# Inputs of the down projection in other buffers, forms and norm products of the feed-forward stage at other places in the order

## The chip, the core and the metric

The kernel runs on one core of one Trainium2 chip. Its engines are TensorE (PE in the profile; its weight loads are listed apart as PEld), VectorE (DVE), ScalarE (ACT) and GpSimd (POOL); SyncE (SP) only issues DMAs, as ScalarE and GpSimd also can. Each engine works through its own list of instructions in order, and waits where an instruction needs what another engine has not finished. The time is the device time of one execution in microseconds, the median of several runs.

## The reference

Two layers of a bidirectional encoder trunk in float32, on 512 tokens of width 1024:

```python
for l in range(DEPTH):                                   # DEPTH = 2
    h = rms_norm(x, attn_norm_g[l])
    proj = h @ w_in[l]
    c_q, c_kv, k_rope, gq, gk, gv, pool_in, gate_logits = split_columns(proj, IN_SIZES)
    o_mla = mla_branch(...)                              # latent attention, 8 heads
    o_gqa = gqa_branch(...)                              # grouped-query attention, 8 heads on 2
    o_pool = pool_branch(...)                            # centred means over 2/4/8/16 tokens
    merged = gates[0] * (o_mla @ w_branch_mla[l]) + gates[1] * (o_gqa @ w_branch_gqa[l]) \
             + gates[2] * (o_pool @ w_branch_pool[l])
    x = x + merged @ w_out[l]
    hf = rms_norm(x, ffn_norm_g[l])
    u = depthwise_conv(hf @ ffn_w_up[l], ffn_conv_w[l], ffn_conv_b[l])   # 1024 -> 2 x 2816, width 3
    u_gate, u_val = u[..., :D_FF], u[..., D_FF:]
    x = x + (silu(u_gate) * u_val) @ ffn_w_down[l]       # 2816 -> 1024
```

`rms_norm(x, g)` is `x * rsqrt(mean(x*x) + 1e-6) * g` over the width.

## The kernel before

**Numbers.** A float32 product is made of three matmuls of a faster format: each operand is split into a high part and the remainder, and `mm3` (L529) multiplies high by high, high by low and low by high into one accumulation in PSUM. So every operand has two tiles: `HH` and `HL` for the normed input, `wh` and `wl` for weights, `act` twice (or `ah` and `al`) for the input of the down projection.

**Order.** Nothing is scheduled by the compiler: the Python code writes every engine's list itself, and the order in which it writes is the order in which each engine works. To choose it, the code keeps a clock (`Clock`): it estimates when each instruction would end, and a chain of steps (`chain(..., after=t)`) is written when the estimated time reaches its place. Whatever has the earlier estimated time stands earlier in an engine's list. The real waits are semaphores.

**Memory.** Tiles lie in pools that are opened one after the other and get their byte offsets in that order. Pool `sp` has 47 plain slots of 2048 bytes per partition for nearly everything; `wp` has 5 wide ones of 2112 bytes (for the means); `sm` has the small ones; `mp` has 4 buffers of 6144 bytes, used in attention and, in the feed-forward stage, as 12 places of 2048 bytes for inputs of the down projection. A slot that is taken again makes its first writer wait for its last reader. In the built program `mp` is last and its places begin at 204640, 206688 and so on, that is at 32 past a multiple of 64 bytes; the plain slots begin at 93824 and lie, like `HH` and `HL`, at multiples of 128; the wide buffers begin at 190080, 192192, 194304, 196416 and 198528, of which the second and the fourth lie 64 past a multiple of 128.

**From the output projection to the feed-forward stage.** The output projection gives 8 columns of 128 features, each an accumulation of 24 matmuls 512 tokens wide (operands `mgh`, `mgl`). Behind each column m a chain stands: VectorE adds it to the residual (`XM`), ScalarE makes `HH` and the squares, VectorE makes `HL`, GpSimd adds the squares. Then the feed-forward stage needs two things of it.

- The norm: `norm_begin` transposes the sum of squares (`sqT`) and reduces it on VectorE (`prt`). `norm_finish` puts one small product of `prt` on TensorE (into `ps_S`), and from it come the factors `fac`, `rt` and the row `rbc` by which results are multiplied later. It is called at every step of the first accumulations, and writes the product at the first call where the estimate says that `prt` has been ready for `D_SUM` (2.0 us; `D_FIRST`, 2.4, for the very first norm, generation 0). Generations 1 and 3 are the two feed-forward norms, 2 is the norm ahead of the second layer.
- The forms: the up projection is made in two ways. The first 5 of 22 chunks are plain (10 accumulations of 24 matmuls 512 wide, 8 row blocks of three). The other 17 use a scheme with seven products in place of eight for each two by two blocks (forms 11, 12, 1, 22, 2, 4, 3), 256 tokens wide. It needs sums and differences of row blocks: `build_forms(q)` for the quad q of row blocks 2q and 2q + 1 scales the two (`hn`), makes four half-wide sums (`tt`) on VectorE, and splits them into `tf`. It is called behind each odd column, and its chain starts 2.0 us of estimated time later.

**Down projection.** The 22 chunks are in five groups of 5, 5, 5, 4 and 3. While one group's forms are multiplied, the products of the group before with the down weights (`act` or `ah`/`al`, 512 wide) are dealt out between them in bursts of some 6 to 9 matmuls. The last group's stand alone at the end of the layer. Of each group, chunks go to the 12 places of `mp` as far as they reach (groups of 5, 1, 5, 1 and 3 chunks, two places each); the other 4 and 3, called the spare ones here, have their high part in a wide buffer (`ah`) and their low part in a plain slot (`al`). 8 columns by 22 chunks make 176 down products of three matmuls in a layer.

Of the kernel before, what the change touches and what calls it, by code (L numbers as in the profile page):

```python
# [11 lines left out]
F32R = mybir.dt.float32r  # L12
# [6 lines left out]
P = 128  # L19
T = 512  # L20
# [10 lines left out]
WIDE = 528  # L31
# [26 lines left out]
D_SUM, D_FIRST = 2.0, 2.4  # L58
# [150 lines left out]
class Clock:  # L209
# [37 lines left out]
    def done(self, *key):  # L247
        self.ready[key] = self.fin + self.SEM

    def need(self, *keys):  # L250
        for k in keys:
            while k not in self.ready:
                self.pop()
            self.to(self.ready[k])
# [4 lines left out]
    def chain(self, *steps, after=0.2):  # L259

        def go(n, source=None):
            if n == len(steps):
                return
            keys, fn = steps[n] if isinstance(steps[n], tuple) else ((), steps[n])
            late = [self.ready.get(k, self.now + 0.5) for k in keys]
            if late and max(late) > self.now:
                self.at(max(late) - self.now, lambda: go(n))
                return
            self.fin, self.source, self.last = self.now, source, None
            fn()  # L270
            source, self.source = self.last, None
            self.at(max(0.0, self.fin - self.now), lambda: go(n + 1, source))
        self.at(after, lambda: go(0))
# [65 lines left out]
def trunk(ctx: ExitStack, tc: tile.TileContext, x, w, prm, gb, cst, out):  # L339
    nc = tc.nc  # L340
    ctx.enter_context(tc.manual_schedule())
    ck = Clock()
    at, need, done, chain = ck.at, ck.need, ck.done, ck.chain
# [3 lines left out]
    cp = ctx.enter_context(tc.tile_pool(name="cp", bufs=1))  # L347
    rawp = ctx.enter_context(tc.tile_pool(name="rawp", bufs=RAW))
    hlp = ctx.enter_context(tc.tile_pool(name="hlp", bufs=LA + 3))
    sp = ctx.enter_context(tc.tile_pool(name="sp", bufs=NSLOT))  # L350
    wp = ctx.enter_context(tc.tile_pool(name="wp", bufs=NWIDE))
    sm = ctx.enter_context(tc.tile_pool(name="sm", bufs=2))
# [3 lines left out]
    uid = [0]  # L356

    def slot(name, dt=F32):
        uid[0] += 1
        t = sp.tile([P, SLOT], dt, tag="s", name=f"{name}_{uid[0]}")  # L360
        return t
# [5 lines left out]
    def small(name, shape, dt=F32, bufs=2):  # L367
        uid[0] += 1
        t = sm.tile(shape, dt, tag=name, name=f"{name}_{uid[0]}", bufs=bufs)
        return t  # L370
# [4 lines left out]
    def ps(tag):  # L375
        while not banks[tag]:
            ck.pop()
        ck.to(heapq.heappop(banks[tag]))
        uid[0] += 1
        t = pp.tile([P, T], F32, tag=tag, name=f"ps_{tag}_{uid[0]}", bufs=nbank[tag])  # L380
        return t
# [8 lines left out]
    def free(tag):  # L390
        heapq.heappush(banks[tag], ck.fin + ck.SEM)

    def f(ap):
        return ap.bitcast(F32)
# [130 lines left out]
    def mm(o, lhsT, rhs, start, stop, again=False):  # L525
        PE.matmul(o, lhsT=lhsT, rhs=rhs, start=start, stop=stop, skip_group_check=again)  # L526
        n = rhs.shape[-1]
        ck.to(ck.now + (n / 2400.0 + 0.0133 if st["ffn"] else max(0.107, n / 2370.0)))
# [20 lines left out]
    keep = cp.tile([P, 1], F32, tag="keep", name="keep")  # L549


    mp = ctx.enter_context(tc.tile_pool(name="mp", bufs=4))

    prms = []
    for l in range(L):
        t = cp.tile([P, NPRM], F32, tag=f"prm{l}", name=f"prm{l}")
# [60 lines left out]

    def norm_finish(gen, out, force=False):

        if gen not in parts or not (force or ck.ready.get(("prt", gen), 1e9) + (D_SUM if gen else D_FIRST) <= ck.now):  # L620
            return
        need(("prt", gen))
        s2 = ps("S")
        mm(s2[:, :16], C[:, C_GRP:C_GRP + P], parts.pop(gen), True, True)
        a, a4 = small("fac", [P, 16]), small("fac4", [P, 16])
        rt, rbc = out["rt"], out["rbc"] = small("rt", [P, 4]), slot("rbc")

        def mean():
            V.tensor_scalar(a, s2[:, :16], 1.0 / D, EPS, ALU.mult, ALU.add)
            free("S")  # L630

        def tokens():
            V.tensor_tensor(a4, a, C[:, C_SEL:C_SEL + 16], ALU.mult)
            V.tensor_reduce(rt, a4.rearrange("p (b g) -> p b g", g=4), AX.X, ALU.add)
            done("rt", gen)

        def rows():
            V.transpose(rbc[:, :T].rearrange("p (j r) -> p j r", r=32), bc(a.unsqueeze(2), [P, 16, 32]))
            done("rbc", gen)

        chain(mean, lambda: G.tensor_tensor(a, a, bc(mhalf, [P, 16]), ALU.pow), tokens, rows, after=0.3)
# [13 lines left out]
    parts = {}  # L655

    def bc(ap, shape):
        return ap.to_broadcast(shape)
# [26 lines left out]
    def layer(l, sq, xsrc):  # L685
# [3 lines left out]
        def col(i):  # L689
            return pr[:, i:i + 1]  # L690
# [899 lines left out]
        def build_forms(q):  # L1590
            a, b = slot("hn")[:, :T], slot("hn")[:, :T]
            lo, hi = slice(0, 256), slice(256, 512)
            t = (slot("tt")[:, :T], slot("tt")[:, :T])

            def whole():
                for k, z in ((2 * q, a), (2 * q + 1, b)):
                    V.tensor_scalar(z, XM[:, k, :], col(PRM_FG + k), None, ALU.mult)

            def sums():
                V.tensor_tensor(t[0][:, lo], a[:, hi], a[:, lo], ALU.subtract)  # L1600
                V.tensor_tensor(t[1][:, lo], b[:, hi], a[:, hi], ALU.subtract)
                V.tensor_tensor(t[0][:, hi], b[:, hi], t[0][:, lo], ALU.subtract)
                V.tensor_tensor(t[1][:, hi], b[:, lo], t[0][:, hi], ALU.subtract)

            def halves_of(name):
                i, h = {"1": (0, lo), "2": (0, hi), "3": (1, lo), "22": (1, hi)}[name]
                d = slot("tf", F32R)[:, :T]
                forms[name, q] = d[:, lo], d[:, hi]

                def low():  # L1610
                    V.tensor_tensor(d[:, hi], t[i][:, h], f(d[:, lo]), ALU.subtract)
                    done("tf", l, name, q)
                return [lambda: A.activation(d[:, lo], t[i][:, h], AF.Copy), low]

            for name, k, h in (("11", 2 * q, lo), ("12", 2 * q + 1, lo), ("4", 2 * q + 1, hi)):
                forms[name, q] = HH[:, k, h], HL[:, k, h]
                done("tf", l, name, q)
            chain(whole, sums, *[z for name in ("1", "2", "22", "3") for z in halves_of(name)], after=2.0)

        for m in range(KC):  # L1620
            tag = tags[m % 3]
# [28 lines left out]
        def keep_act(c):  # L1650
            g = next(i for i, (c0, c1) in enumerate(groups) if c0 <= c < c1)
            i = c - groups[g][0]
            n = 2 * (PLACE[g] + i)
            if n < 2 * ROOM:
                return places[n], places[n + 1]
            uid[0] += 1
            return wp.tile([P, WIDE], F32R, tag="w", name=f"ah_{uid[0]}")[:, :T], slot("al", F32R)[:, :T]

        def convolve(c, part, u):
            ci = c + part * FC  # L1660
# [353 lines left out]
```

## Time and profile before

| | us |
|---|---|
| median of 3 runs (lowest, highest) | 1552.65 (1552.56, 1552.98) |
| the profiled execution, device time | 1550.6 |
| its span, first to last instruction | 1548.8 |
| TensorE busy | 1542.1 |
| VectorE, ScalarE, GpSimd busy | 1156.3, 1066.5, 775.3 |
| granted TensorE clock, mean | 1.000 |

In a row of a timeline the first number is the start in us from the span's start, the second the duration of the row's instructions, then engine, line, operation, and output tile <- input tiles with their shapes; in brackets stands the idle time just before and what ended it. Matmuls overlap in the pipeline: a 512-wide one lasts 0.39 us, but the next starts some 0.23 us after it. So the distance from start to start is what counts. In a view of groups the two numbers behind the bar are the busy time in us and the mean duration of one in ns; in a view of waits they are the total, the number of times and the longest.

### The profile page before, as it was taken

To read this page: it belongs to the slowest core of one execution; us is meant where nothing else is said; L and a number is where in the kernel's file an instruction comes from. 1 tells how busy PE (TensorE), PEld (TensorE's weight loads), DVE (VectorE), ACT (ScalarE), POOL (GpSimd) and SP (SyncE) were. 2 spreads that over 40 slices of the span, in tenths; PEclk is the share of its full clock that TensorE was granted. 3 is DMA by queue.
4 is the path that set the end of the run, shared out by engine and by line. 5 is a ranking of instruction groups with operands and counts; after the bars stand their busy time and mean duration, and the time that the engine had idled before them with its cause. 6 is when DMAs were issued, how large, how long until landed. Compare 5 with 4: busy or idle time off the path is not lost.

```text
span 1548.8 us, 24353 instructions
## 1 busy us (share of the span) xinstructions
PE 1542.1 (100%) x8265; PEld 1341.3 (87%) x8265; DVE 1156.3 (75%) x1936; ACT 1066.5 (69%) x1994; POOL 775.3 (50%) x828
## 2 busy tenths in 40 slices
PE   9999999999999999999999999999999999999999
PEld 8888888888878999999898888888888899999997
DVE  6877886776687887877756678868667778888785
ACT  5557875877657877777644577758776677777772
POOL 3984886753453323222488648776535432222223
PEclk9999999999999999999999999999999999999999
DMA  5432344658968878886434323447598688787853
GB/s 203 123 120 82 88 123 141 162 128 207 225 164 195 197 169 181 197 192 143 128 128 131 111 75 92 125 144 175 117 216 213 169 205 186 180 187 177 212 116 102
DMA packets 138509, 241.26 MB, mean 156 GB/s; under 512 B 30864, under 2 KB 53392, under 8 KB 138384
## 3 DMA queue, kind: packets, MB, share of 16 engines
q1 hardware_dynamic: 91152, 162.93, 34.0%
q0 software_dynamic: 42336, 76.56, 28.8%
q8 instruction: 65, 1.06, 0.3%
q10 hardware_dynamic: 4896, 0.21, 0.2%
q14 instruction: 60, 0.49, 0.1%
HBM read 149.41 MB, written 13.63 MB: 105 GB/s over the span
## 4 chain that ended last, share of the span: by engine, by line
PE 92%; DVE 3%; DMA 2%; ACT 1%; issue 1%; POOL 1%; SPq 0%; ACTq 0%; POOLq 0%; DVEq 0%
PE ps_acc L526 40%; PE ps_AV L526 17%; PE ps_ST L526 15%; PE ps_S L526 10%; PE ps_mi L526 9%; DMA raw<-w 1%; DVE tf L307 1%; ACT wh L300 0%; SPq L862 0%; POOL wl L307 0%; DVE ctl L311 0%; DVE win L307 0%; ACT mx L300 0%; DVE wl L307 0%; POOL fac L307 0%
## 5 line engine op out<-in xcount | busy, mean ns | idle before, releaser
L438 POOL DMA_DIRECT2D wl<-raw x192 | 172.4, 903 | 383.1 <-ACT sx L300 163.7
L307 POOL TENSOR_TENSOR wl<-raw,wh 128x512 fp32r<-128x512 f32 (+2 forms) x171 | 219.9, 1294 | 179.4 <-ACT wh L300 171.7
L300 ACT ACTIVATE wh<-raw 128x512 fp32r<-128x512 f32 (+2 forms) x453 | 266.3, 605 | 55.6 <-DMA raw<-w 13.2
L438 POOL DMA_DIRECT2D fl<-raw x102 | 89.0, 873 | 155.2 <-ACT fl L300 62.6
L526 PE MATMUL ps_acc<-HH,wh 128*128 128x512 f32 x416 | 163.2, 392 | 0.5 <-DVE XM L311 0.4
L526 PE MATMUL ps_acc<-HL,wh 128*128 128x512 f32 x416 | 162.8, 391 | 0.3 <-DVE HL L311 0.3
L526 PE MATMUL ps_acc<-HH,wl 128*128 128x512 f32 x416 | 162.7, 391 | 0.0
L311 DVE SCALAR_TENSOR_TENSOR a<-u,prm,a 128x511 f32<-128x511 f32 x176 | 133.5, 761 | 33.5 <-ACT a L300 32.5
L300 ACT ACTIVATE wl<-wh 128x512 fp32r<-128x512 f32 x192 | 120.6, 628 | 6.1
L315 DVE TENSOR_REDUCE nm<-ps_S 128x1 fp32r<-128x512 f32 x128 | 87.8, 686 | 44.6 <-PE ps_S L526 43.7
L300 ACT ACTIVATE a<-u,prm 128x512 f32<-128x512 f32 x88 | 71.2, 811 | 57.2 <-DVE u L307 57.1
L526 PE MATMUL ps_acc<-tf,wh 128*128 128x256 f32 x544 | 100.1, 282 | 0.0
L526 PEld LDWEIGHTS ps_acc<-tf,wh 128*128 128x128 f32 x544 | 88.5, 189 | 6.2
L526 PEld LDWEIGHTS ps_acc<-HH,wh 128*128 128x128 f32 x416 | 78.4, 188 | 16.6 <-issue 0.7
L526 PEld LDWEIGHTS ps_acc<-HH,wl 128*128 128x128 f32 x416 | 78.2, 188 | 16.8
L526 PEld LDWEIGHTS ps_acc<-HL,wh 128*128 128x128 f32 x416 | 78.3, 188 | 16.6 <-DVE HL L311 0.6
L307 DVE TENSOR_TENSOR wl<-raw,wh 128x512 fp32r<-128x512 f32 (+2 forms) x91 | 66.2, 729 | 22.9 <-ACT wh L300 22.7
L526 PE MATMUL ps_AV<-HH,wh 128*128 128x256 f32 (+1 forms) x248 | 82.2, 331 | 0.0
L526 PE MATMUL ps_AV<-HH,wl 128*128 128x256 f32 (+1 forms) x248 | 82.1, 331 | 0.0
L526 PE MATMUL ps_AV<-HL,wh 128*128 128x256 f32 (+1 forms) x248 | 82.1, 331 | 0.0
L526 PE MATMUL ps_acc<-tf,wl 128*128 128x256 f32 x272 | 76.7, 282 | 0.0
L307 DVE TENSOR_TENSOR pl<-ps_ST,ph 128x512 fp32r<-128x512 f32 x86 | 58.3, 682 | 15.6 <-ACT ph L300 11.4
(426 smaller groups left out, 4975.3 us busy)
## 6 DMA issues: line engine op xcount, KB each, us to landing
raw<-w SPq DMA_DIRECT2D x160, 512.0 KB, 3.9
wl<-raw POOLq DMA_DIRECT2D x188, 256.0 KB, 4.4
raw<-w SPq DMA_DIRECT2D x140, 256.0 KB, 4.4
fl<-raw POOLq DMA_DIRECT2D x102, 256.0 KB, 5.6
raw<-w SPq DMA_DIRECT2D x14, 384.0 KB, 3.0
XM<-x SPq DMA_DIRECT2D x16, 256.0 KB, 4.5
dtq<-tr SPq DMA_DIRECT2D x16, 192.0 KB, 2.0
dtk<-tr SPq DMA_DIRECT2D x16, 192.0 KB, 3.3
```

Source lines behind the costliest of these rows:

```text
L300: return self.eng.activation(out, in_, func, **k)
L307: return self.eng.tensor_tensor(out, *a)
L311: return self.eng.scalar_tensor_tensor(out, *a)
L315: return self.eng.tensor_reduce(out, in_, *a, **k)
L438: nc.gpsimd.dma_start(f(lo), r, accum_op=ALU.add)
L526: PE.matmul(o, lhsT=lhsT, rhs=rhs, start=start, stop=stop, skip_group_check=again)
```

## The change

It has four edits in three parts. `mp` is opened ahead of the plain slots; in the built program its places then begin at 93824, 95872 and so on, all at multiples of 128, and the plain slots behind it at 118400, also at multiples of 128. The spare chunks' high parts (`ah`) go to plain slots too. The product of a feed-forward norm (generations 1 and 3) is written once `prt` has been ready for 2.4 us of estimated time, not 2.0. And the chain of `build_forms` starts 8.0 us after the norm step for quads 2 and 3, not 2.0.

```diff
     hlp = ctx.enter_context(tc.tile_pool(name="hlp", bufs=LA + 3))
+    mp = ctx.enter_context(tc.tile_pool(name="mp", bufs=4))
     sp = ctx.enter_context(tc.tile_pool(name="sp", bufs=NSLOT))
...
-    mp = ctx.enter_context(tc.tile_pool(name="mp", bufs=4))
-
...
     def norm_finish(gen, out, force=False):
 
-        if gen not in parts or not (force or ck.ready.get(("prt", gen), 1e9) + (D_SUM if gen else D_FIRST) <= ck.now):
+        if gen not in parts or not (force or ck.ready.get(("prt", gen), 1e9) + (D_FIRST if gen in (0, 1, 3) else D_SUM) <= ck.now):
             return
...
-            chain(whole, sums, *[z for name in ("1", "2", "22", "3") for z in halves_of(name)], after=2.0)
+            chain(whole, sums, *[z for name in ("1", "2", "22", "3") for z in halves_of(name)], after=2.0 if q < 2 else 8.0)
...
             if n < 2 * ROOM:
                 return places[n], places[n + 1]
-            uid[0] += 1
-            return wp.tile([P, WIDE], F32R, tag="w", name=f"ah_{uid[0]}")[:, :T], slot("al", F32R)[:, :T]
+            return slot("ah", F32R)[:, :T], slot("al", F32R)[:, :T]
```

What moves, first on VectorE, at the end of the first layer's output projection. `XM<-ps_ST` is the residual of the last column, `HL` the low part of a normed row block, `hn`, `tt` and `tf` belong to the third quad's forms, `sqT` and `prt` to the norm. Before:

```order
L311 SCALAR_TENSOR_TENSOR XM<-ps_acc_4604,XM 128x512
L311 SCALAR_TENSOR_TENSOR HL<-XM,prm_91,HH 128x512
L319 TENSOR_SCALAR hn_4671<-XM,prm_91 128x512
L319 TENSOR_SCALAR hn_4672<-XM,prm_91 128x512
L307 TENSOR_TENSOR tt_4673<-hn_4671 128x256
L307 TENSOR_TENSOR tt_4674<-hn_4672,hn_4671 128x256
L307 TENSOR_TENSOR tt_4673<-hn_4672,tt_4673 128x256
L307 TENSOR_TENSOR tt_4674<-hn_4672,tt_4673 128x256
L311 SCALAR_TENSOR_TENSOR XM<-ps_ST_4660,XM 128x512
L307 TENSOR_TENSOR tf_4675<-tt_4673,tf_4675 128x256
L311 SCALAR_TENSOR_TENSOR HL<-XM,prm_91,HH 128x512
```

And now:

```order
L311 SCALAR_TENSOR_TENSOR XM<-ps_acc_4604,XM 128x512
L311 SCALAR_TENSOR_TENSOR HL<-XM,prm_91,HH 128x512
L311 SCALAR_TENSOR_TENSOR XM<-ps_ST_4660,XM 128x512
L311 SCALAR_TENSOR_TENSOR HL<-XM,prm_91,HH 128x512
L319 TENSOR_SCALAR hn_4671<-XM,prm_91 128x512
L319 TENSOR_SCALAR hn_4672<-XM,prm_91 128x512
L307 TENSOR_TENSOR tt_4673<-hn_4671 128x256
L307 TENSOR_TENSOR tt_4674<-hn_4672,hn_4671 128x256
L307 TENSOR_TENSOR tt_4673<-hn_4672,tt_4673 128x256
L307 TENSOR_TENSOR tt_4674<-hn_4672,tt_4673 128x256
L331 STREAM_TRANSPOSE sqT_4712<-sq_4307 128x512
L315 TENSOR_REDUCE prt_4713<-sqT_4712 128x16
```

The residual and the low part of the last row block now stand ahead of the third quad's scalings and sums, and the norm's transpose and reduction ahead of that quad's four `tf`. The second layer shows the same.

On TensorE, in the second accumulation of the feed-forward stage, `ps_S<-prt` is the norm's product. Before:

```order
L526 MATMUL ps_ST_4778<-HH,wl_4691 128x512
L526 MATMUL ps_S_4814<-prt_4719,C 128x16
L526 MATMUL ps_ST_4778<-HH,wh_4690 128x512
L526 MATMUL ps_ST_4778<-HL,wh_4690 128x512
L526 MATMUL ps_ST_4778<-HH,wl_4691 128x512
```

And now:

```order
L527 MATMUL ps_ST_4770<-HL,wh_4690 128x512
L527 MATMUL ps_ST_4770<-HH,wl_4691 128x512
L527 MATMUL ps_S_4813<-prt_4713,C 128x16
L527 MATMUL ps_ST_4770<-HH,wh_4690 128x512
L527 MATMUL ps_ST_4770<-HL,wh_4690 128x512
L527 MATMUL ps_ST_4770<-HH,wl_4691 128x512
```

Two more row blocks, six matmuls, now stand ahead of the product, with one row block behind it in the accumulation where there were three. Apart from the product, TensorE's list is the same throughout; GpSimd's and SyncE's lists are the same; ScalarE's changes only at the same two places, where the next weight splits now come ahead of the forms' copies.

## The prediction

> **What bounds the kernel now.** I read the page first (engines, granted clock, chain), then the view of waits for TensorE, then the timelines of TensorE, VectorE and ScalarE around the two places where a feed-forward stage begins, then TensorE's groups by shape in the down projections, and last the load queue.
>
> ```profile
> span 1548.8 us, 24353 instructions
> PE 1542.1 (100%) x8265; PEld 1341.3 (87%) x8265; DVE 1156.3 (75%) x1936; ACT 1066.5 (69%) x1994; POOL 775.3 (50%) x828
> PE 92%; DVE 3%; DMA 2%; ACT 1%; issue 1%; POOL 1%; SPq 0%; ACTq 0%; POOLq 0%; DVEq 0%
> ```
>
> The reader is to see that TensorE is the bound: it is busy over the whole span and makes up 92% of the chain that ended last. A change moves the time only where it closes a gap between two matmuls, or shortens the distance from one matmul's start to the next. The view of waits (total, times, longest) names the gaps near this change:
>
> ```profile
> PE ps_S L526 <- DVE prt L315: 0.6, 2, 0.4
> PE ps_acc L526 <- DVE HL L311: 0.3, 1, 0.3
> ```
>
> The one wait for `HL` is in the first layer: the last row block (7) of the normed input comes late to the first feed-forward accumulation. TensorE there, start of each matmul in the first column:
>
> ```profile
> 425.67 0.39 PE L526 MATMUL ps_ST<-mgh,wh 128*128 128x512 f32 x1
> ...
> 426.12 0.39 PE L526 MATMUL ps_ST<-mgh,wl 128*128 128x512 f32 x1
> ...
> 430.43 0.39 PE L526 MATMUL ps_acc<-HH,wh 128*128 128x512 f32 x1
> ...
> 432.19 0.50 PE L526 MATMUL ps_acc<-HL,wh 128*128 128x512 f32 x1 [0.28 <-DVE HL L311]
> ...
> 432.77 0.39 PE L526 MATMUL ps_ST<-HH,wh 128*128 128x512 f32 x1
> ```
>
> From 425.67 to 430.43 lie 21 matmuls: 4.76 / 21 = 0.2267 us from start to start, the undisturbed distance of a 512-wide matmul here. From 430.43 to 432.77 lie six, which should take 1.36 us and take 2.34: 0.98 us are lost.
>
> **Part 1, forms of the later quads scaled 8.0 after the norm step, not 2.0.** Nothing is added; VectorE's order changes. Why `HL` was late:
>
> ```profile
> 425.46 0.88 DVE L319 TENSOR_SCALAR hn<-XM,prm 128x512 f32<-128x512 f32 x2
> 426.26 1.52 DVE L307 TENSOR_TENSOR tt<-hn 128x256 f32<-128x256 f32 x1
> 427.70 1.51 DVE L307 TENSOR_TENSOR tt<-hn,hn 128x256 f32<-128x256 f32 x1
> 429.13 0.87 DVE L307 TENSOR_TENSOR tt<-hn,tt 128x256 f32<-128x256 f32 x2
> 429.92 0.68 DVE L311 SCALAR_TENSOR_TENSOR XM<-ps_ST,XM 128x512 f32<-128x512 f32 x1
> ...
> 431.39 0.75 DVE L311 SCALAR_TENSOR_TENSOR HL<-XM,prm,HH 128x512 fp32r<-128x512 f32 x1 [0.46 <-ACT HH L300]
> ...
> 434.95 0.70 DVE L331 STREAM_TRANSPOSE sqT<-sq 128x512 f32<-128x512 f32 x1
> ...
> 435.89 0.67 DVE L315 TENSOR_REDUCE prt<-sqT 128x16 f32<-128x512 f32 x1
> ...
> 437.27 0.41 DVE L307 TENSOR_TENSOR tt<-hn 128x256 f32<-128x256 f32 x1
> ```
>
> ```profile
> 430.63 0.72 ACT L300 ACTIVATE HH<-XM,prm 128x512 fp32r<-128x512 f32 x1 [2.35 <-DVE XM L311]
> ```
>
> The last column of the output projection ends on TensorE at 426.12 + 0.39 = 426.51, but VectorE first does the third quad's six instructions (425.46 to 429.92) and only then the residual. In the changed order the residual stands ahead of them: 426.51 + 0.68 (residual) + 0.72 (`HH` on ScalarE) + 0.75 (`HL`) = 428.7, with hand-overs 428.9. TensorE wants row block 7 three matmuls after 430.43, at 431.1, so 2.2 us are to spare and the whole 0.98 us goes. In the second layer the view of waits has no such wait, and nothing is gained. What is late next: the forms themselves, some 3.5 us later. Their first reader is the second group's products, a whole group of 240 matmuls of 0.2267 us (54 us) later; that is the cover. Without it each late form would stop TensorE for its own lateness. ScalarE's next weight splits now stand ahead of the forms' copies, which only helps the weights; POOL's and SP's queues keep their order.
>
> **Part 2, the norm's product two row blocks later.** In the two feed-forward norms it stands six matmuls (1.36 us) later on TensorE.
>
> ```profile
> 435.95 0.39 PE L526 MATMUL ps_ST<-HH,wl 128*128 128x512 f32 x1
> 436.61 0.40 PE L526 MATMUL ps_S<-prt,C 128*128 128x16 f32 x2 [0.27 <-DVE prt L315]
> 436.85 0.48 PE L526 MATMUL ps_ST<-HH,wh 128*128 128x512 f32 x1
> ```
>
> ```profile
> 1205.13 0.39 PE L526 MATMUL ps_ST<-HH,wl 128*128 128x512 f32 x1
> ...
> 1205.81 0.48 PE L526 MATMUL ps_ST<-HH,wh 128*128 128x512 f32 x1
> ```
>
> ```profile
> 793.42 0.40 PE L526 MATMUL ps_AV<-HH,wl 128*128 128x512 f32 x1
> ...
> 793.79 0.48 PE L526 MATMUL ps_AV<-HH,wh 128*128 128x512 f32 x1
> ```
>
> The third block is the same product where its input had long been there: 0.37 us from the matmul ahead of it to the one behind. Here it takes 0.90 and 0.68, so 0.53 + 0.31 = 0.84 us are waits for `prt`. After the change, first layer: TensorE comes to the product at 435.95 + 0.23 - 0.98 + 1.36 = 436.6. `prt` is ready at 428.9 + 0.88 (two scalings) + 3.90 (four sums, at the slow durations above) + 0.70 + 0.67 = 435.0 at the latest, POOL's sum of squares lying beside the forms. Second layer: 769.2 later for TensorE less the 0.98 it never lost, 1206.7 against 1205.2. All 0.84 us go; the ends are 0 and 0.84. What comes later is the row `rbc`, by 1.36 us; the first bank it must free is needed six accumulations of 24 matmuls (5.4 us each) after the first began, at some 459, which hides it.
>
> The sums' duration is itself a question of neighbours: 1.52 us here, 0.41 for its like at 437.27. The Trainium skill (SBUF — State Buffer, "Who interferes with whom") says that a VectorE instruction with two SBUF inputs contends with a GpSimd instruction that reads SBUF; the trace agrees, and I have taken the slow value above.
>
> **Part 3, the inputs of the down projections at other byte offsets.** The 12 kept tiles of a layer begin at 32 past a multiple of 64 bytes before and at multiples of 128 after. The spare high parts sat in the wide buffers, at multiples of 128 or 64 past one, and move to plain slots, all at multiples of 128. No instruction is added. The last group of the second layer is a run of `act` matmuls alone:
>
> ```profile
> 1528.38 0.63 PE L526 MATMUL ps_acc<-act,wh 128*128 128x512 f32 x2
> ...
> 1543.08 0.40 PE L526 MATMUL ps_mi<-act,wh 128*128 128x256 f32 x2
> ```
>
> Seven columns of three chunks of three matmuls are 63: 14.70 / 63 = 0.2333 us, 6.6 ns over the 0.2267 of `mgh` and `HH`, which lie at multiples of 128. The first layer's last group reads alike:
>
> ```profile
> L526 PE MATMUL ps_acc<-act,wh 128*128 128x512 f32 x18 | 5.7, 395 | 0.0
> ```
>
> If the offset is the cause, 63 + 72 such matmuls win 135 x 6.6 ns = 0.89 us. Between the form products, where down matmuls come in bursts behind 256-wide ones, the distance is less clean. Between 695 and 750 us all spare parts lie at multiples of 128:
>
> ```profile
> L526 PE MATMUL ps_mi<-act,wh 128*128 128x512 f32 x16 | 5.0, 396 | 0.0
> L526 PE MATMUL ps_mi<-al,wh 128*128 128x512 f32 x9 | 3.6, 395 | 0.0
> L526 PE MATMUL ps_mi<-ah,wl 128*128 128x512 f32 x9 | 3.5, 392 | 0.0
> L526 PE MATMUL ps_mi<-ah,wh 128*128 128x512 f32 x9 | 3.5, 392 | 0.0
> L526 PE MATMUL ps_mi<-act,wl 128*128 128x512 f32 x8 | 3.1, 393 | 0.0
> ```
>
> A product of three is 396 + 396 + 393 = 1185 ns from `act` and 392 + 395 + 392 = 1179 from the spare ones: 6 ns. Part of that is place: the kept chunk tends to come first in a burst. I take half, 3 ns, for the 192 kept products per run that lie in bursts: 0.58 us; the ends are 0 and 192 x 3 x 6.6 ns = 3.8 us. The 32 products with a spare high part 64 past: 0.1 us, ends 0 and 0.4.
>
> The Trainium skill speaks against this part: SBUF — State Buffer ("Door 1", its note) gives cachelines of 16 bytes, and 96, 64 and 0 are all whole lines. TensorE: Matmul & The Clock Gate ("Back-to-back issue gap") makes the distance a matter of width alone. By these pages the part would be worth nothing and the sum 1.8 us. The trace has 0.2333 against 0.2267 us at one width, and the measurement decides unless something else differs between the two runs (second rival).
>
> **The sum.** 0.98 + 0.84 + 0.89 + 0.58 + 0.10 = 3.4 us. The profiled execution took 1550.6 us, 1.8 around its span; the median of the runs is 1552.65, and all five terms are stretches that every run has. 1552.65 - 3.4 = 1549.2 us, 0.22% faster. A difference of 0.2% (3.1 us, 1549.5) is about what a measurement of this kernel can tell from none.
>
> **Rivals.**
>
> Second: the offset is indifferent, and the longer distance belongs to the stage. That is what the two pages would have. For it: in attention an operand at a multiple of 128 reads as long as `act`:
>
> ```profile
> L526 PE MATMUL ps_AV<-ph,vg 128*128 128x512 f32 x64 | 25.3, 396 | 0.0
> ```
>
> Against: there each such matmul stands between others of other shapes, whereas the last `act` run is as uniform as the `mgh` run and still longer throughout. Only the waits go: 1552.65 - 1.8 = 1550.8.
>
> Third: bursts win in full: 0.98 + 0.84 + 0.89 + 3.8 + 0.4 = 6.9 us, 1545.7. Against: spare parts at multiples of 128 still read 392 to 395, not 389.
>
> Fourth: the product still waits, because VectorE takes the forms more slowly yet: 0.98 + 1.57 = 2.5 us, 1550.1.
>
> Fifth, slower: plain slots run short. Eight slots instead of four are held by spare chunks, and the weight loads on SP wait for slots already (first block, between 482 and 770 us). Then the loads of one chunk, their first use, and the landing of `raw`:
>
> ```profile
> SPq L407 <- DVE s L307: 17.4, 5, 4.7
> ```
>
> ```profile
> 580.31 9.41 SPq L407 DMA_DIRECT2D raw<-w  x5
> ```
>
> ```profile
> 612.17 0.62 ACT L300 ACTIVATE fh<-raw 128x512 fp32r<-128x512 f32 x1
> ```
>
> ```profile
> DMA to landing us min/median/max: 2.6/4.8/8.4
> ```
>
> The lead is 31.9 us. Landing (8.4 at most), a split and its own transfer of like length leave about 14 us. Up to there a later slot costs nothing; beyond it each of the 14 spare chunks stops TensorE. To end 0.2% slower, 3.1 + 3.4 = 6.5 us must be lost, 0.46 us at each: 1555.8. Everything behind a blocked load on SP waits too, the down weights first.
>
> **Chances.** First case 0.58, second 0.13, third 0.13, fourth 0.07, fifth 0.07, others 0.02. Of the first, seven in ten lie under 1549.5. Faster: 0.41 + 0.13 = 0.54; slower 0.08; same 0.38. The range runs from the third case to a little over the second, 1545.6 to 1551.3, and leaves out the fifth and some of the third. The first case's own range is 1548.2 to 1550.2.
>
> **What will show it.** TensorE's starts from the fourth row block of the first feed-forward accumulation evenly 0.2267 us apart in layer one; the product at 0.37 us in both layers; the last `act` run at 0.2267 us and mean 389; `act` in the bursts near 392. A wait of TensorE for `fl`, `wl` or `raw` near 550 to 640 us would be the fifth case, flat 0.2333 in the last run the second.

## The result, and the profile after

The changed kernel takes 1547.21 us (median of 6 runs, 1546.64 to 1547.71) against 1552.61 us of the kernel before, run beside it. The ratio is 0.9967, with a 95% interval from 0.9955 to 0.9979: 5.4 us or 0.33% faster, where 3.4 us were forecast. The profiled execution took 1547.71 us with a span of 1545.9 us.

The page of the changed kernel:

```profile
span 1545.9 us, 24337 instructions
PE 1538.4 (100%) x8265; PEld 1340.8 (87%) x8265; DVE 1154.5 (75%) x1936; ACT 1066.7 (69%) x1994; POOL 773.8 (50%) x828
PE 92%; DVE 2%; DMA 2%; ACT 1%; issue 1%; POOL 1%; SPq 0%; ACTq 0%; POOLq 0%; DVEq 0%
```

TensorE is the bound as before, and its busy time is shorter by 3.7 us with the same 8265 matmuls: the distances became shorter, not only the gaps. TensorE's timeline at the start of the feed-forward stage, first layer, then second:

```profile
426.49 0.39 PE L527 MATMUL ps_acc<-HH,wh 128*128 128x512 f32 x1
...
431.93 0.39 PE L527 MATMUL ps_ST<-HH,wh 128*128 128x512 f32 x1
...
436.47 0.39 PE L527 MATMUL ps_ST<-HH,wl 128*128 128x512 f32 x1
436.69 0.29 PE L527 MATMUL ps_S<-prt,C 128*128 128x16 f32 x2
436.83 0.48 PE L527 MATMUL ps_ST<-HH,wh 128*128 128x512 f32 x1
...
1204.89 0.39 PE L527 MATMUL ps_ST<-HH,wl 128*128 128x512 f32 x1
1205.12 0.29 PE L527 MATMUL ps_S<-prt,C 128*128 128x16 f32 x2
1205.26 0.48 PE L527 MATMUL ps_ST<-HH,wh 128*128 128x512 f32 x1
```

The 24 matmuls from 426.49 to 431.93 are 0.2267 us apart, and from the matmul ahead of the product to the one behind it pass 0.36 us in the first layer and 0.37 in the second: the waits are gone. VectorE in front of it, first layer:

```profile
426.69 0.69 DVE L311 SCALAR_TENSOR_TENSOR XM<-ps_ST,XM 128x512 f32<-128x512 f32 x1 [1.51 <-PE ps_ST L527]
428.18 0.75 DVE L311 SCALAR_TENSOR_TENSOR HL<-XM,prm,HH 128x512 fp32r<-128x512 f32 x1 [0.79 <-ACT HH L300]
428.85 3.38 DVE L319 TENSOR_SCALAR hn<-XM,prm 128x512 f32<-128x512 f32 x2
432.15 0.41 DVE L307 TENSOR_TENSOR tt<-hn 128x256 f32<-128x256 f32 x1
...
434.34 0.69 DVE L315 TENSOR_REDUCE prt<-sqT 128x16 f32<-128x512 f32 x1
```

`HL` is done at 428.93, forecast 428.9. `prt` is done at 435.03, forecast 435.0, but that hit is luck: the two scalings took 3.38 us where the forecast had 0.88, and the four sums 1.69 (0.41, 0.41 and 0.87 for two) where it had 3.90. TensorE's groups in the last run of the first layer (753 to 778 us), then between the form products (692 to 747 us):

```profile
L527 PE MATMUL ps_acc<-act,wh 128*128 128x512 f32 x18 | 5.6, 390 | 0.0
L527 PE MATMUL ps_acc<-act,wl 128*128 128x512 f32 x9 | 3.5, 389 | 0.0
```

```profile
L527 PE MATMUL ps_mi<-act,wh 128*128 128x512 f32 x16 | 5.0, 395 | 0.0
L527 PE MATMUL ps_mi<-ah,wh 128*128 128x512 f32 x9 | 3.6, 396 | 0.0
L527 PE MATMUL ps_mi<-al,wh 128*128 128x512 f32 x9 | 3.6, 395 | 0.0
L527 PE MATMUL ps_mi<-ah,wl 128*128 128x512 f32 x9 | 3.5, 389 | 0.0
L527 PE MATMUL ps_mi<-act,wl 128*128 128x512 f32 x8 | 3.1, 390 | 0.0
```

395 became 390 in the run; in the bursts the third matmul of each product gained (392 and 393 before), the first two did not. The view of waits for the load queue (480 to 768 us) and the landing of `raw` (540 to 640 us) speak against the fifth rival: loads wait a little more for slots of `s` (21.7 us for 17.4), and TensorE has no wait between 425 and 800 us.

```profile
SPq L408 <- DVE s L307: 21.7, 9, 5.1
```

```profile
DMA to landing us min/median/max: 2.5/4.0/7.2
```

A table by stage shows where the time went. It is made from the timelines' starts: "plain" reaches from the last matmul of the output projection to the first form product that reads a sum, `tf` (484.01 - 426.27 = 57.74 for the first layer of the changed kernel; two form products of the first chunk, which read `HH` and `HL` alone, lie ahead of it and count as plain), "forms" to the last form product, "run" to the last down product. Layers one / two, in us; the runs not yet named come in the next section:

| kernel | plain | forms | run |
|---|---|---|---|
| before, first profile | 59.31 / 58.09 | 267.06 / 266.91 | 23.59 / 23.81 |
| before, second profile | 59.33 / 60.60 | 267.15 / 266.85 | 23.60 / 23.81 |
| offsets alone | 60.39 / 59.92 | 266.76 / 266.27 | 23.09 / 23.34 |
| order alone | 57.75 / 58.33 | 266.67 / 266.85 | 23.60 / 23.81 |
| changed, first profile | 57.75 / 57.91 | 266.26 / 266.26 | 23.08 / 23.29 |
| changed, second profile | 57.75 / 57.97 | 266.26 / 266.26 | 23.08 / 23.30 |

The two profiles of the kernel before differ by 2.5 us in one place, the second layer's plain part. That is most of the 2.9 us by which the two profiled executions differ (spans of 1551.7 and 1548.8 us). The prediction worked from the shorter one, 2.0 us under the median.

### The profile page after: what moved, and what is told of

Read it like the earlier page. It is cut to its first block, busy times and chain, and to the rows that moved or that the text cites. A ratio compares the mean times of both kernels' runs of the same rounds, so it can differ in the third digit from the quotient of the medians.

```text
span 1545.9 us, 24337 instructions
## 1 busy us (share of the span) xinstructions
PE 1538.4 (100%) x8265; PEld 1340.8 (87%) x8265; DVE 1154.5 (75%) x1936; ACT 1066.7 (69%) x1994; POOL 773.8 (50%) x828
## 4 chain that ended last, share of the span: by engine, by line
PE 92%; DVE 2%; DMA 2%; ACT 1%; issue 1%; POOL 1%; SPq 0%; ACTq 0%; POOLq 0%; DVEq 0%
PE ps_acc L527 40%; PE ps_AV L527 17%; PE ps_ST L527 16%; PE ps_S L527 10%; PE ps_mi L527 9%; DMA raw<-w 1%; ACT wh L300 0%; DMA qa<-nm 0%; SPq L861 0%; POOL wl L307 0%; DMA qb<-nm 0%; DVE ctl L311 0%; DVE win L307 0%; ACT mx L300 0%; DVE nm L315 0%
```

## The experiments

**The two parts apart.** Four kernels ran on one chip: the kernel before once more, the buffers alone, the order alone, and the changed kernel once more. The edits are those of the change:

```diff
# e1_offsets: before, and
+    mp = ctx.enter_context(tc.tile_pool(name="mp", bufs=4))
     sp = ctx.enter_context(tc.tile_pool(name="sp", bufs=NSLOT))
...
+            return slot("ah", F32R)[:, :T], slot("al", F32R)[:, :T]
# e2_order: before, and
+ ... + (D_FIRST if gen in (0, 1, 3) else D_SUM) <= ck.now
+ ... for z in halves_of(name)], after=2.0 if q < 2 else 8.0)
```

> The kernel before, unchanged, as one more entry. It shows how far two series of one kernel lie apart and gives a second profile of it. Its one profile so far took 1550.6 us, 2.0 less than the median. Expected: within 1 us of the kernel before. If the second profile is near 1552.6, the rows in which it is longer than the first say where the 2 us lie that no term of the sum holds.

> The offset part alone: kept places at multiples of 128 and spare high parts in plain slots; order as before. Theory (offsets are worth what the two traces show in the feed-forward stages, some 0.9 us in the pure runs and 1.0 between the form products): 1.6 to 2.0 us faster, near 1550.8, and all waits for HL and prt of before still there. Rival (the measured 5.4 us has a further gain from the places, in attention or from other slots): 3.5 us or more faster. Rival (offset indifferent): within 0.5 us of before.

> The order part alone: forms of quads 2 and 3 scaled 8.0 behind, norm products two row blocks later; all buffers as before. Theory: the waits of the two starts go, 1.8 us, near 1550.8; the last run of act matmuls stays at 0.2333 us. Rival (what the sum lacks lies in the order, in work that the moved forms no longer disturb): 3.5 us or more faster.

> The changed kernel, unchanged, beside its two parts on one chip. Theory (two independent parts): the gains of the two parts add up to its own within 1 us, and it is 3.4 to 4 us faster than before. Rival (the parts help each other): its gain exceeds their sum by more than 1 us. Its second profile tells whether the wait for qa near 1018 us, which the first profile has and before has not, belongs to the change (it would be there again) or to that one execution.

| kernel | median, us | ratio to before, 95% interval |
|---|---|---|
| before again | 1551.98 | 1.0000 (0.9991 to 1.0009) |
| offsets alone | 1549.06 | 0.9985 (0.9977 to 0.9994) |
| order alone | 1548.74 | 0.9980 (0.9971 to 0.9989) |
| changed again | 1546.66 | 0.9968 (0.9957 to 0.9979) |

By the ratios 2.3 and 3.1 us, together 5.4, against 5.0 for both, where 3.4 to 4 were expected. The parts add up as far as intervals of 1.2 to 1.7 us to either side can tell, and nothing is seen of the rival that they help each other; in the table by stage the offsets gain 2.0 us in forms and runs both without the order part (against the second profile of before) and on top of it. The offset part is what was expected within its interval. The order part is worth nearly twice the 1.8 us, between its theory and its rival. The second profile of the kernel before says why. Waits for TensorE between 1190 and 1256 us, where its first profile has none:

```profile
PE ps_acc L526 <- DMA wl<-raw: 0.6, 1, 0.6
PE ps_acc L526 <- ACT HH L300: 0.5, 1, 0.5
PE ps_acc L526 <- DVE HL L311: 0.3, 1, 0.3
PE ps_S L526 <- DVE prt L315: 0.3, 1, 0.3
```

VectorE and GpSimd there, first profile, then second:

```profile
1196.06 2.60 POOL L307 TENSOR_TENSOR wl<-raw,wh 128x512 fp32r<-128x512 f32 x1 [1.95 <-ACT wh L300]
1196.42 0.42 DVE L307 TENSOR_TENSOR tt<-hn 128x256 f32<-128x256 f32 x1
...
1200.34 0.75 DVE L311 SCALAR_TENSOR_TENSOR HL<-XM,prm,HH 128x512 fp32r<-128x512 f32 x1
```

```profile
1196.87 1.60 POOL L307 TENSOR_TENSOR wl<-raw,wh 128x512 fp32r<-128x512 f32 x1 [1.93 <-ACT wh L300]
1197.23 1.52 DVE L307 TENSOR_TENSOR tt<-hn 128x256 f32<-128x256 f32 x1
1198.68 1.51 DVE L307 TENSOR_TENSOR tt<-hn,hn 128x256 f32<-128x256 f32 x1
...
1202.38 0.75 DVE L311 SCALAR_TENSOR_TENSOR HL<-XM,prm,HH 128x512 fp32r<-128x512 f32 x1 [0.46 <-ACT HH L300]
```

The same instructions run beside each other, and either GpSimd is held up (2.60 us, VectorE's first sum 0.42) or VectorE is (1.52 and 1.51, GpSimd 1.60). In the first case `HL` is in time, in the second it stops TensorE. The old order is at the mercy of that. In the new one the sums come after `HL`, and none of the profiles with the new order has a wait for `HL` or `prt` at these two places. The kernel with the buffers alone shows the same waits in both layers, longer yet in the first (1.1 us for `HH`). The wait for `qa` near 1018 us in the first profile of the changed kernel was not there again.

**Which offset counts.** Six kept tiles of each layer's last group were put at other starts, in tiles 32 bytes longer:

```diff
+MIX = ((0, 4, 8, 0, 4, 8), (0, 4, 8, 1, 2, 2))
+SWAP = ((0, 1, 2), (0, 1))
...
-            t = mp.tile([P, 3, T], F32R, tag="m", name=f"act{l}{n}")
-            places += [t[:, k, :] for k in range(3)]
+            t = mp.tile([P, 3 * T + 8], F32R, tag="m", name=f"act{l}{n}")
+            for k in range(3):
+                o = T * k + (MIX[l][3 * n + k] if n < 2 else 0)
+                places.append(t[:, o:o + T])
...
-                return places[n], places[n + 1]
+                k = n // 2 in SWAP[l]
+                return places[n + k], places[n + 1 - k]
```

> The changed kernel, but the six kept tiles of each layer's last group start at different bytes past a multiple of 128. First layer, high and low part of its three chunks: 16 and 0, 64 and 32, 96 and 80; second layer: 112 and 96, 4 and 0, 8 and 8. The runs of down products alone then read, chunk by chunk, the price of an offset. Theory (a 512-wide operand costs 6.6 ns more if it does not start at a multiple of 128 bytes, whatever the rest): 233.3 ns from start to start for every high and low part but the two zeros, so triples near 693 with a zero in them and near 700 without. Rival (multiples of 64 are free): triples with 64 as high part near 687. Rival (whole lines of 16 bytes are free, as the Trainium skill, SBUF, has the cachelines): 16, 32, 64, 80, 96, 112 free, near 680, and only 4 and 8 dear. Rival (price grows with the offset): 112 dearer than 16.

The products in the last runs took, in the mean, by start of high and low part past a multiple of 128: 16 and 0: 694 ns; 64 and 32: 696; 96 and 80: 697; 8 and 8: 698; 112 and 96: 704; 4 and 0: 711. The changed kernel has some 682, the kernel before 699 to 700. So multiples of 16 and of 64 are not free, and the price does not simply grow with the offset: 112 and 96 are dearer than 16 and 0, but 8 and 8 are dearer than 64 and 32. But the theory fell too. The one execution took 1556.06 us, some 9 more than the changed kernel, mostly because the longer tiles had moved all plain slots by 128 bytes. Groups of the output projection (375 to 430 us) and of the plain accumulations (437 to 484 us) in this run:

```profile
L529 PE MATMUL ps_acc<-mgh,wh 128*128 128x512 f32 x24 | 9.5, 395 | 0.0
...
L529 PE MATMUL ps_AV<-HH,wh 128*128 128x512 f32 x24 | 9.3, 389 | 0.0
```

`mgh` now began at multiples of 256, which are multiples of 128, and read 395 where it had read 389: from start to start 44.57 / 191 = 0.2333 us, not 0.2267. What had changed was its place against the weights, which stayed. In both given kernels weights, `HH` and plain slots all begin 128 past a multiple of 512. (The low part called 0 in the pair of 4 and 0 began 256 past one, so no matmul of that dearest product began like its weights.) So the next kernel moved the weights, the kept places and the slots by 128 bytes together and left only `HH` and `HL`:

```diff
+    pad = ctx.enter_context(tc.tile_pool(name="pad", bufs=1))
+    pad.tile([P, 32], F32, tag="pad", name="pad")
     hlp = ctx.enter_context(tc.tile_pool(name="hlp", bufs=LA + 3))
```

> The changed kernel with 128 unused bytes ahead of the weight tiles, so that weights, kept places and plain slots all begin at 256 past a multiple of 512 bytes and only HH and HL stay where they were, at 128 past. In the run with mixed offsets mgh, mgl, oh and ol stood at multiples of 256, as did no weight, and took 229 and 237 ns in turn, 233.4 in the mean, although multiples of 128; in the changed kernel moving operand and weights stand at 128 past a multiple of 512, both. Theory (what counts is that moving operand and weights begin alike): mgh and the last act runs keep 226.7 ns, and HH and HL, now unlike their weights, go to some 233 in the plain up projection and the input projection; the kernel some 10 us slower. Rival (the moving operand alone counts, and has to begin at an odd multiple of 128): mgh and act go to 233, HH stays at 226.7. Rival (the weights alone count): both go to 233.

The groups of the same places, and of the last run:

```profile
L529 PE MATMUL ps_acc<-mgh,wh 128*128 128x512 f32 x24 | 9.3, 389 | 0.0
...
L529 PE MATMUL ps_AV<-HH,wh 128*128 128x512 f32 x24 | 9.5, 395 | 0.0
...
L529 PE MATMUL ps_acc<-act,wh 128*128 128x512 f32 x18 | 5.5, 389 | 0.0
```

`mgh` and `act` are back at 389 beside weights that moved with them, and `HH`, which had not moved, is the slow one: 395. Both rivals fall, since each of the two operands was the fast kind in one kernel and the slow kind in another at the same start. What counts here is that the moving operand and the weights begin at the same place modulo 512 bytes (or 256: the runs don't tell these apart, and starts that differ by 256 were not tried in a run of matmuls alone). The one execution took 1555.59 us, 8.4 to 8.9 more than the changed kernel, as expected. Form products 256 wide keep 120 ns in the mean either way. The mechanism behind it stays open.

**The order part taken apart.** Product alone, forms alone, and the changed kernel with the product put back:

```diff
# e5_product_alone: before, and
+ ... + (D_FIRST if gen in (0, 1, 3) else D_SUM) <= ck.now
# e10_forms_alone: before, and
+ ... for z in halves_of(name)], after=2.0 if q < 2 else 8.0)
# e12_product_back: changed, and
+ ... + (D_SUM if gen else D_FIRST) <= ck.now
```

> The kernel before with the norm products two row blocks later, and nothing else. Theory (the 3.1 to 3.5 us of the order part are mostly the late HL of both layers, which the moved forms cure; the product is worth what its waits were, some 0.5 us in each layer): 0.5 to 1.1 us faster, and the waits for HL stay. Rival (the product's place is what matters): 2.5 us or more faster. Rival (prt comes later than the product even so): no difference.

> The kernel before with the forms of quads 2 and 3 scaled 8.0 behind the norm step, and nothing else; the norm product stays at its old place. Product alone was 3.3 us slower than before, both together 3.1 us faster. Theory (the late product delays fac and the weights that GpSimd sends behind it only where prt comes late; with the forms out of the way prt is early, so that the product's place costs and brings little): 2.5 to 3.5 us faster, like both together. Rival (the later product costs its 3.3 us in both): 6 us faster. Rival (the moved forms help only together with the later product): under 1 us faster.

> The changed kernel with the norm product at its old place; forms and offsets as changed. Without the forms' move the later product cost 3.3 us, on top of it it won 2.2 (0.998 against 0.9994 of before). Theory (with the forms out of the way prt is early at either place, but the product's place also decides whether ScalarE writes the weight splits ahead of or behind the steps on the first chunks; where they stand behind, TensorE waits for wl near 460 us): 1 to 2.5 us slower than the changed kernel, 1548 to 1549.5, with waits for wl and none for prt in the feed-forward stages. Rival (as the prediction had it, the waits of the product itself): the product waits for prt, 0.5 us in the first layer. Rival (the difference between the two earlier runs was chance): same as the changed kernel within 0.7 us.

| kernel | median, us | ratio to before, 95% interval |
|---|---|---|
| product alone | 1556.78 | 1.0021 (1.0013 to 1.0030) |
| forms alone | 1551.47 | 0.9994 (0.9985 to 1.0003) |
| both (order alone, above) | 1548.74 | 0.9980 (0.9971 to 0.9989) |
| changed, product back | 1548.44 | 0.9980 (0.9971 to 0.9989) |

The product alone makes the kernel 3.3 us slower, which none of its three theories had. The longest wait of TensorE in that kernel, and its place in the second layer:

```profile
PE ps_acc L526 <- DMA wl<-raw: 2.9, 2, 2.5
```

```profile
1235.94 0.80 PE L526 MATMUL ps_acc<-HH,wl 128*128 128x512 f32 x1 [2.49 <-DMA wl<-raw]
1236.54 0.63 PE L526 MATMUL ps_acc<-HH,wh 128*128 128x512 f32 x1
```

A wait of 1.8 us for `prt` near 30 us in this profile belongs to the very first norm, which the edit leaves alone. The chain behind the wait for `wl`, in the same kernel on VectorE and ScalarE:

```profile
1208.63 0.87 DVE L319 TENSOR_SCALAR hn<-XM,prm 128x512 f32<-128x512 f32 x2
...
1211.21 0.17 DVE L319 TENSOR_SCALAR fac<-ps_S 128x16 f32<-128x16 f32 x1
...
1215.94 0.70 DVE L331 STREAM_TRANSPOSE rbc<-fac 128x512 f32<-128x512 f32 x1
```

```profile
1217.59 1.52 ACT L300 ACTIVATE a<-u,prm 128x512 f32<-128x512 f32 x2 [4.16 <-DVE u L307]
...
1231.12 0.63 ACT L300 ACTIVATE act<-a 128x512 fp32r<-128x512 f32 x1 [2.33 <-DVE a L307]
1231.66 1.14 ACT L300 ACTIVATE wh<-raw 128x512 fp32r<-128x512 f32 x2
```

With the forms still early in the order, `prt` is late; the product that waits for it is written later, the fourth quad's forms slip in ahead of `fac`, and `rbc` is done at 1216.6. In the kernel with both edits `rbc` is done at 1210.85, and its plain part began only 3.5 us earlier, so `rbc` is 2.3 us late. Against the second profile of the kernel before it is only 0.4 us late (18.9 us behind the last matmul of the output projection for 18.4), so most of the loss against that kernel arises after `rbc`. On ScalarE the steps `a` and `act` of the first chunks, which need `rbc`, stand ahead of weight splits. ScalarE stands 4.16 us for the first of them, the later ones follow in a chain with VectorE, and the split at 1231.66, behind such a step, comes too late: TensorE ends a matmul at 1233.45 and waits for its `wl`. This wait and the slow matmuls after it (last section) hold the 3.3 us by which this second plain part, 63.88 us, exceeds that of the second profile of before. That the order on ScalarE is the cause is read from this one profile.

With the forms moved, `fac` is early, and the later product is then a gain in the plain parts: putting it back in the changed kernel makes them 1.2 us longer in all (58.43 and 58.52 us, against 57.75 and 57.97). The change moves more on ScalarE than splits past the forms' copies: with both edits a weight split also stands ahead of the first step `a`; with the product at its old place that `a` stands ahead of the split. The medians differ by 1.2 to 1.8 us, as expected, but the intervals overlap, and the profiled execution, 1546.63 us, is no longer than the changed kernel's second, 1546.66, since its attention was shorter by as much. Its waits are for weights, as expected, none for `prt` in the feed-forward stages:

```profile
PE ps_acc L527 <- DMA wl<-raw: 0.8, 2, 0.5
```

The forms alone won 0.9 us, with an interval from a gain of 2.3 to a loss of 0.5. By the median that is not the theory's 2.5 to 3.5 but the under 1 us of the second rival, by which the moved forms help only together with the later product; the interval leaves room between the two. Its one profile has lost the waits for `HL` and `prt` in both layers and has 0.8 us of waits for `wl` instead. Its two feed-forward stages are 0.9 us shorter than in the first profile of before and 3.4 us shorter than in the second; how its other executions spend their time was not seen.

**Slots.** The fifth rival, tried from its own side with `NSLOT = 44` for 47:

> The changed kernel with 44 plain slots instead of 47, against the fifth rival (slots run short). Theory (the loads of weights have room to spare): loads of raw start later, up to some 10 us, but TensorE has no new wait for fl, wl or raw between 550 and 640 us, and the time stays within 1 us of the changed kernel. Rival (47 was already at the edge): waits of TensorE for fl or wl in the products, 3 us or more in all.

In the feed-forward stages the theory held: no wait of TensorE between 480 and 770 us, the forms stages 266.26 us both. But the kernel took 1560.65 us in its one execution, 14 us more than the changed kernel. The loss lies in attention, 7.6 us in the first layer and 6.6 in the second, and 7.7 of the 14 us are waits for `nm`:

```profile
PE ps_S L527 <- DVE nm L315: 7.7, 8, 2.6
```

So three slots fewer are too few, only not where the rival looked.

**Longer bursts.** In the changed kernel a burst of six down matmuls with the 20 form matmuls around it takes 3780 ns (five bursts of each layer), nine take 4460 (four of each): 20 ns more than the undisturbed distances of 226.7 and 120 give, whatever the length. So fewer bursts should pay:

```diff
-SPOTS = ("22", "2", "4", "3")
+SPOTS = ("2", "3")        # e7_longer_bursts
+SPOTS = ("3",)            # e11_one_burst
```

> The changed kernel with the down products dealt out behind two of the seven form products and not four, so in half as many bursts of twice the length (12 to 18 matmuls). In the changed kernel a burst and the 14 form matmuls behind it take 20 ns more than their matmuls undisturbed (227 and 120 ns each), at six matmuls as at nine. Theory (the change of width costs, not the matmul): 34 bursts a layer fewer x 2 x 20 ns = 1.4 us faster than the changed kernel, 6.8 us faster than before. Rival (products that follow each other without a burst wait for the copies out of PSUM, or for weights): slower than the changed kernel, with new waits of TensorE for sx, u, fl or wl.

> The changed kernel with all down products of a chunk behind the last of its seven form products: one burst of 24 matmuls where the kernel with longer bursts has two. There, from the first form product to the last down product, a layer took 288.7 and 288.9 us against 289.3 and 289.55 in the changed kernel, 0.65 less for 34 bursts fewer. Theory (each change of width costs 20 ns): 17 bursts fewer, 0.3 us a layer less again, 288.4 and 288.6; the kernel some 2 us faster than the changed kernel. Rival (seven form products in a row outrun the copies or the weights): that stretch longer than 289.3 us, with waits of TensorE for fl, wl or sx.

Two bursts: 1546.56 us, ratio 0.9958 (0.9946 to 0.9970). From the first form product with a sum to the last down product the first layer takes 773.14 - 484.45 = 288.69 us; the changed kernel takes 289.34:

```profile
484.45 0.40 PE L527 MATMUL ps_AV<-tf,wh 128*128 128x256 f32 x2
...
773.14 0.39 PE L527 MATMUL ps_ST<-act,wl 128*128 128x512 f32 x1
```

```profile
484.01 0.40 PE L527 MATMUL ps_AV<-tf,wh 128*128 128x256 f32 x2
...
773.35 0.39 PE L527 MATMUL ps_ST<-act,wl 128*128 128x512 f32 x1
```

0.65 us of the 0.68 expected, and 0.64 in the second layer. It is the fastest of all kernels by its ratio, though its interval overlaps that of the changed kernel and its median is only 0.1 to 0.7 us lower. One burst: 1559.49 us, ratio 1.0054 (1.0040 to 1.0067). The same stretch takes 295.80 and 295.76 us, 6.5 and 6.2 more than in the changed kernel. Seven form products in a row outrun the copies out of PSUM, as the rival had it; these two waits are 7.5 of the 12.7 us:

```profile
PE ps_acc L527 <- ACT sx L300: 4.6, 6, 0.9
PE ps_AV L527 <- ACT sx L300: 2.9, 3, 1.3
```

## Why the prediction was right, and where it was not

The direction was right and the size was low: 3.4 us forecast, 5.4 measured, and the measured time, 1547.21, lies within the range but outside the first case's own (1548.2 to 1550.2). Step by step:

- **Part 1, first layer (0.98 us).** Right, with its times: `HL` done at 428.93 for 428.9. Together with the product's 0.53 the plain part fell by 1.57 us, forecast 1.51.
- **Part 1, second layer ("nothing is gained").** Wrong, and the largest miss. The view of waits was right for that one execution only. In the second profile of the kernel before, the plain part of the second layer lost 2.5 us more than in the first profile, 1.6 of it at `HL` and `prt` and 0.9 at weights. The prediction had seen that the sums take 0.41 or 1.52 us by what runs beside them, and had not asked of the second layer what happens if they take 1.52.
- **Part 2 (0.84 us).** The waits for `prt` went, but not because the product stands later: in the profiles of forms alone and of the changed kernel with the product put back they are gone too. So the reason given failed: Part 1 alone ends these waits. The prediction's own numbers say so for the first layer: at the old place TensorE would have come at 435.95 + 0.23 - 0.98 = 435.2, with `prt` ready at 435.0. And that `prt` came when it was forecast is luck, as said above. The product's worth beside the moved forms is some 1.2 us in the plain parts, through the order of ScalarE's splits and the steps `a`. The step "what comes later is the row `rbc`, by 1.36 us; the first bank hides it" looked at the wrong reader. Banks are hidden; ScalarE's list is not. With the product alone `rbc` came 2.3 us later than with both edits, and the kernel lost 3.3 us against before.
- **Part 3, last runs (0.89 us).** Right: the 135 matmuls of the sum went from 0.2332 to 0.2272 us from start to start, some 0.8 us. The runs as the table cuts them hold 213 down matmuls and fell by 0.52 us in each layer.
- **Part 3, bursts and spare parts (0.58 + 0.10).** Low: the forms stages fell by 0.41 and 0.59 us against the order alone, 1.0 us. "Near 392" was wrong as a picture: the first two matmuls of a product stayed near 395, the third fell to 390. The eight bursts of nine in a layer gained 28 ns each (4488 to 4460 with the matmuls around them), 0.23 us of it; those of six from kept chunks gained 2 ns, those with spare parts between -9 and 20.
- **Part 3, its cause.** "Multiples of 128" is refuted as the rule: at multiples of 256 the same operand was slow beside weights that were not. The change helped because 93824 and 118400 lie as the weights do, 128 past a multiple of 512. Of the five wide buffers only the first did; 194304 and 198528, multiples of 128, did not. For the spare parts in the bursts this rule is not shown: the bursts that lost 9 ns had their high parts in the first and the third wide buffer.
- **Not in the sum.** A wait for `fl` near 500 us, 0.4 us in the first layer, went with the order part.
- **Rivals.** The second (offset indifferent) falls by the last runs and by the two kernels with other starts, and with it what the two pages of the Trainium skill named there would make of this case. The third (bursts in full) falls by the bursts, though the total of 5.4 us lies between it and the first case. The fourth did not happen: VectorE took the scalings more slowly, but the sums faster, and the product did not wait. The fifth falls for the feed-forward stage.

By the profiles the parts come to 4.3 us (order, against the second profile: 1.58 + 2.27 in the plain parts, 0.48 at `fl`) and 2.0 us (offsets); by the medians to 3.1 and 2.3. The difference in the order part is within its interval (1.7 to 4.5 us), and the old order's second layer, whose plain part is 0.2 or 2.7 us longer than the changed kernel's by the execution, is enough for it.

## What to carry to other kernels

A wait that one profile does not show may be there in the next execution: where a duration has two values by what runs beside it, price the place with both, and take a second profile when the profiled execution lies 2 us off the median. Of a step that is moved later, ask not only which bank or buffer needs its result but which instructions of other engines stand in line behind those that need it. And compare the start of TensorE's moving operand with the start of its weights: here a difference of 128 bytes cost 6.7 ns on each 512-wide matmul in an unbroken run, 3%, and it can come from a pool that was opened in another order.

## What the runs showed of the hardware that was not expected

- The distance of 512-wide matmuls was 226.7 ns where moving operand and weights began alike modulo 512 bytes and 233.4 ns where they began 128 bytes apart. The products with mixed starts, up to 128 bytes away, had 231 to 237 ns in the mean, the most (711 / 3) with differences of 4 and 128. In the run with mixed offsets `mgh` and `mgl` beside their unlike weights took some 229 and 237 ns in turn.
- A change of width costs 20 ns for a burst in all, there and back, where everything begins alike (3780 ns for 3760 undisturbed, 4460 for 4440).
- In the kernel with the product alone two matmuls started 2.88 us apart for want of `wl`; the next ones stood 0.43 us apart, not 0.227, for some 2.7 us, and the granted clock there was 0.50:

```profile
1235.90:1238.50 2.60, 2.56 (x6) 2.08 (x7) 0.44 (x1) 2.57 (x5) 1.28 (x1) 0.50 0.81 215
```

  (stretch, its length, then busy time and count of TensorE, its weight loads, VectorE, ScalarE and GpSimd, then the clock, the DMA share and GB/s.) In the kernel with 44 slots two idle times of TensorE of 2.61 us, near 167 and 942 us, were followed by a granted clock of 0.53 and 0.51 over the next 3.5 us. An idle time of 1.84 us near 30 us of the kernel with the product alone left the clock at 1.00. So this wait cost some 1.2 us more than itself (six distances of 0.427 for 0.227). The Trainium skill (TensorE: Matmul & The Clock Gate, "Part 1: The HAM clock gate") has the clock halved after an idle window of about 3.4 us; here an idle time of 2.49 us was enough.
